# Thirteen dual products and four plain gate blocks in a gated convolution block: the lead computes products 1 and 2 of two duals

## The chip, the cores and the metric

The kernel runs on one core of a Trainium2 chip (trn2). The metric is the device time of one execution in microseconds (us); the time of a kernel is the median of several runs. Beside the runs stands one profiled execution, with a record of every instruction: TensorE (PE) does the matrix products and has its weight loads shown apart (PEld), VectorE (DVE), ScalarE (ACT) and GpSimd (POOL) work on elements, and the sync engine (SP) issues most transfers.

## The reference, cut to what matters

```python
h = rms_norm(x, norm_mix_g) * (1.0 + sc1) + sh1
proj = einsum('bsd,de->bse', h, w_in)            # 1024 x 1024 by 1024 x 7168
b_s, c_s, v_s, v_c, gl_c, gate_br = split(proj)  # 56 blocks of 128 columns
y_a = b_s * causal_dwconv(c_s * v_s, conv_short_w)          # width 3
u = v_c * sigmoid(gl_c)
u = causal_dwconv(u, conv_conf_w) + conv_conf_b             # width 31
g_a, g_b = split(sigmoid(gate_br))
...
```

After it come two projections, the gated merge, an output projection, a SwiGLU layer and a last norm. None of these is touched by the change. The stage in question is the input projection `proj`: 1024 tokens (two halves of 512), 1024 input channels (8 chunks of 128, `KC`), and 56 blocks of 128 output channels: 8 each of `bs`, `cc`, `vs`, `vc`, `gl`, and the gates `ga` and `gb`.

## The kernel before

All data stand channel-major: a tile has 128 channels on the partitions and 512 tokens. A float32 product is made of three matmuls of a rounded format: each operand is split into a rounded part and a rest (`wh`, `wl` of a weight; names ending in `h`, `l` of an operand), and `mm3` issues `wh` by `xh`, `wh` by `xl`, `wl` by `xh`. One such triple multiplies a 128 by 128 weight with 512 tokens. The rounded part is made on ScalarE (L226 for weights, L420, L470 for operands), the rest on VectorE or GpSimd (L227, L421, L471).

**The lead.** The first blocks of the projection run while the inputs are still being normalised. `row_blocks` keeps seven output banks open (`LEAD` = 7: three pairs `gl`, `vc` and the gate `gb` 0) and loops over the chunks k of the input. For each k, `act_x` loads two modulation rows (`modulation`, a VectorE reduction L361), scales x (`modulate`: VectorE L462, ScalarE L470 makes `hk0h`, VectorE L471 `hk0l`), and seven outputs get their products with that chunk. In the first half of the tokens (h = 0) chunks 0 to 2 are whole float32 products (`WHOLE` = 3, L376), and chunks 3 to 7 are triples, 21 matmuls a chunk. After chunk 6's second output the sum of squares of the second half, `ss`, is made on TensorE (`SUM_AT`, L540) from `squares_x` (ScalarE L525, VectorE L529); its reciprocal root scales the second half. The second half of the lead (h = 1) takes the chunks in the order 5, 6, 7, 0, 1, 2, 3, 4, with 7 x 3 matmuls a chunk. At the end of a half `glu` and `gate` empty the banks.

**One plain block** (`gb` 1, 48 matmuls) follows, by `col_block`.

**The duals.** The remaining 48 blocks are done in pairs, two pairs a dual (`PAIRS`), by a 2 by 2 scheme of Winograd's kind: seven products (`PRODUCTS` = "1265734", in this order) in place of eight. Products 1 and 2 use the plain operands (`th["1"]`, `th["2"]` are chunks 0 to 3 and 4 to 7 of the first half), the others sums and differences of operands (`t2`, `t`: VectorE L425, L712, L718, split by `t_split`) and of weights. One product is 2 output blocks x 4 chunks x 3 = 24 matmuls. The weights of a dual come from `dual_units`: all seven are split on GpSimd (wl, L227), and the four sums of weights are GpSimd's too. `win_evac` empties the banks; with it, eight 31-tap convolutions (`conv`, L915) run on VectorE, spread over `CONV_DUALS` duals.

What decides the order: the kernel is traced in program order, and a list scheduler with modelled times gives each engine one queue; `issue_after` adds edges to it. On the chip each queue is taken in its order, and an instruction waits for semaphores of others. `keep_clock` puts fillers on TensorE during the start (`CLOCK`). `raws` are five buffers for weight loads, in turn.

Of the kernel before, what the change touches and what calls it, by code (L numbers as in the profile page):

```python
# [40 lines left out]
P = 128  # L41
# [23 lines left out]

LEAD = 7
WHOLE = 3

CLOCK = (10, 3, (5,), 9, 5)

# [20 lines left out]
PAIRS = [  # L94
# [4 lines left out]
]  # L99


CONV_DUALS = 11

# [24 lines left out]
def block_kernel(ctx: ExitStack, tc: tile.TileContext, x0, xT, c, vecs, ada, w_first, w_plain, w_duals,  # L128
# [81 lines left out]
    def load(src, n=1024):  # L210
        raw = raw_tile(n)
        load.ins = nc.sync.dma_start(raw, src).ins
        return raw

    pool_los = []
# [81 lines left out]

    def apart_units(mats, eng):


        a = {}

        def add(out, x, y):
            eng.tensor_tensor(out, x, y, ALU.add)
            return out

        def get(b):
            return load(mats[("11", "12", "21", "22").index(b)])

        def unit(m):  # L310
            if m in "12":
                raw = get("1" + m)
            elif m == "6":
                for b in ("21", "22", "11"):
                    a[b] = get(b)
                a["s1"] = add(a["22"], a["21"], a["22"])
                raw = a["s2"] = add(raw_tile(), a["11"], a["s1"])
            elif m == "7":
                raw = add(a["21"], a["21"], a["11"])
# [5 lines left out]
            return split_w(raw, 1024, (), eng)  # L325
# [46 lines left out]
    def mm3(outs, wsl, w, xs, first, last, again=False):  # L372

        if w[1] is None:
            for ps, x in zip(outs, xs):
                mm3.ins = nc.tensor.matmul(ps, w[0][:, wsl], x, start=first, stop=last).ins  # L376
            return
        wh, wl = w[0][:, wsl], w[1][:, wsl]
        for ps, (xh, xl) in zip(outs, xs):
            nc.tensor.matmul(ps, wh, xh, start=first, stop=False, skip_group_check=again)  # L380
            nc.tensor.matmul(ps, wh, xl, start=False, stop=False, skip_group_check=again)  # L381
        for ps, (xh, _) in zip(outs, xs):
            mm3.ins = nc.tensor.matmul(ps, wl, xh, start=False, stop=last, skip_group_check=again).ins  # L383
# [113 lines left out]

    def row_blocks(act, n, name, ops, unit, joined=2):

# [3 lines left out]
        for k in range(KC):  # L503
# [51 lines left out]
    def glu(j, h, gl, vc):  # L555
        if h == 0:
            u.append(u_tile(j))
        sig = g_tile("sig")
        nc.scalar.activation(sig, gl, AF.Sigmoid)
        nc.vector.tensor_tensor(u[j][:, CK - 1 + h * H : CK - 1 + (h + 1) * H], vc, sig, ALU.mult)  # L560

# [84 lines left out]
    def act_x(k, h=0):  # L646
        nonlocal rx_0, rx_1
        if h == 0:
            with ExitStack() as after:
                after.enter_context(tc.issue_after(squares_x.ins[1] if k in (0, X1_AT + 2) else modulate.ins[0]))  # L650
                for i in range(2 * k, 2 * k + 2):
# [6 lines left out]
        hT[k][h] = modulate(x[k, h], rx_1 if h else rx_0, naff1[:, k : k + 1], modc(k),  # L658
                            None if whole else f"h{k}{h}", None if h else xin[k])
        if h == 0:  # L660
            if k == X1_AT:
                for i in range(KC):
                    x[i, 1] = s_tile(f"x{i}1")
                    nc.sync.dma_start(x[i, 1], xT[i, :, halves[1]])
            elif k == X1_AT + 1:
# [5 lines left out]
            if whole:  # L671
                return x[k, 0]
        elif k < WHOLE:
            hT[k][0] = split(x[k, 0], hl_tile, f"h{k}0")
        return hT[k][h]

    def sum_x1():
# [15 lines left out]
    rx_1 = None  # L693
    plan[:KC] = [lambda k=k: weights(w_first[k], LEAD * P, [modulate.ins[0]]) for k in SECOND[KEPT:]]
    ops = ()
    for h in range(2):
        lead = row_blocks(act_x if h == 0 else lambda i: act_x(SECOND[i], 1), LEAD, "lead", ops,
                          again_w if h else lead_w, 1 + h)
        if h == 0:
            ops = [(again_w(i), xs) for i, xs in ((i, act_x(SECOND[i], 1)) for i in range(2))]  # L700
        for j in range(LEAD // 2):
            glu(j, h, lead[2 * j], lead[2 * j + 1])
        gate("b", 0, h, lead[-1])


    KH = KC // 2
    th = {m: [None] * KH for m in PRODUCTS}
    t2 = []
    for k in range(KH):
        (b11, b12), (b21, b22) = ((x[i, 0], x[i, 1]) for i in (k, k + KH))  # L710
        th["1"][k], th["2"][k], th["3"][k] = hT[k][0], hT[k + KH][0], hT[k + KH][1]
        nc.vector.tensor_tensor(b11, b11, b12, ALU.subtract)  # L712
        t2 = hl_tile("t2", dt=F32)
        minus(t2, b11, b22)
        th["6"][k] = t_pair("t2")
        t_split(t2, *th["6"][k])
        minus(b21, t2, b21)
        nc.vector.tensor_tensor(b12, b22, b12, ALU.subtract)  # L718
    for h, ps in enumerate(col_block(next_w(), hT, (0, 1), "gb")):
        gate("b", 1, h, ps)  # L720
    for m, i, h in (("5", 0, 0), ("7", 0, 1), ("4", KH, 0)):
        for k in range(KH):
            th[m][k] = t_pair("t")
            t_split(x[k + i, h], *th[m][k])


# [19 lines left out]

    reads = [(0.0, t_split.ins)]

# [18 lines left out]
    def win_evac(d, pairs, banks):  # L767
# [23 lines left out]
        def read(i, m, ps):  # L791
            kind, j, *rest = pairs[i]
            e = st[i]
            if m in "165":
                if m == "5":
                    e["z"] = e["c"][1] if kind == "g" else g_tile("z")
                copy = nc.scalar.copy({"1": banks["y", i], "6": e.get("b", [0, 0])[1], "5": e.get("z")}[m], ps)
                if i:
# [42 lines left out]
        return evac  # L841


# [50 lines left out]
    TAPS = CK // 2 * 3 + 2  # L894

    def read_at(t):

        return max((r for r in reads if r[0] <= t), key=lambda r: r[0])[1]

    def conv(j):  # L900
# [3 lines left out]
        d, e = diff[:, :NE], diff[:, NE : 2 * NE - 1]  # L904
        with tc.issue_after(read_at(j * CONV_DUALS / KC)):
            nc.vector.tensor_tensor(d, ev, od, ALU.subtract)
# [4 lines left out]
        def tap(out, src, s, wt, acc):  # L911
            nonlocal n
            n += 1
            with tc.issue_after(read_at((j * TAPS + n) * CONV_DUALS / (KC * TAPS))):
# [4 lines left out]
        with tc.issue_after(read_at(j * CONV_DUALS / KC)):  # L919
            nc.vector.tensor_scalar(a0, od[:, :H], wsum[:, j : j + 1], col(V_CB, j), ALU.mult, ALU.add)  # L920
# [8 lines left out]
    def add_conv(j):  # L929

        hi, lo = pool_los[min(int((j + 1) * CONV_DUALS * 7 / KC) + 5, 7 * n_duals - 1)]
        with tc.issue_after(hi):
# [40 lines left out]

    n_duals = len(PAIRS) // 2
    ring = [[ps_tile("bank") for _ in range(2)] for _ in "xyz"]
    for d in range(n_duals):
        banks = {(b, p): ring[(d + i) % 3][p] for i, b in enumerate("xyz") for p in range(2)}
        evac = win_evac(d, PAIRS[2 * d : 2 * d + 2], banks)
        if d == n_duals - 1:
            q_steps.pop(0)()  # L980
        for i, m in enumerate(PRODUCTS):
            product(banks, m, th[m], evac, onto="2")
            if d == n_duals - 1:
                q_steps.pop(0)()
    while late:
# [564 lines left out]
```

## Time and profile before

| | |
|---|---|
| median of 3 runs | 1472.15 us (1470.73 to 1473.96) |
| the profiled execution | 1470.4 us, its span 1468.6 us |
| matmuls, VectorE, ScalarE, GpSimd instructions | 6443, 1627, 895, 464 |
| weights of the duals (`in_w_duals`) | 48 loads of 512 KB, 3.5 us each to landing |

The span is the time from the first to the last recorded instruction. The stretches are: start until 16 us, whole products of the lead to 34 us, the first half of the lead to 59 us, the second half to 97 us, the plain block to 108 us, and then the duals until about 565 us. In the rows of the timeline, columns are the start in us, the duration in us, engine, line, operation, output<-inputs, shapes and count; in square brackets stands the idle time of the engine before it and what ended it. A row with a count above 1 covers several instructions, and its duration reaches from the first one's start to the last one's end. "Windows" rows give the busy time of each engine with the number of instructions in a stretch, then the granted TensorE clock and the transfers.

### The profile page before, as it was taken

The page shows a single profiled execution, that of the slowest core. Times are in us where ns is not written, and L with a number is a line of the kernel's source. Part 1 is how long each engine was busy: PE and PEld are TensorE (multiplying, and loading weights), DVE is VectorE, ACT ScalarE, POOL GpSimd, SP SyncE. Part 2 cuts the span into 40 slices and gives each one's busy share as a digit, 9 for nine tenths or more (in the row PEclk, how much of TensorE's full clock was granted, in tenths as well). Part 3 has the DMA queues.
Part 4 walks back from the last instruction along what each step waited for, and adds up shares of the span by engine and source line. Part 5 has one row for each costly group of instructions (what it writes and reads, how often), then busy time and mean ns, then how long its engine had stood idle before and what let it go on. Part 6 is the DMA issues. An engine that isn't in the chain of part 4 may idle for free.

```text
span 1468.6 us, 17760 instructions
## 1 busy us (share of the span) xinstructions
PE 1457.7 (99%) x6443; PEld 1197.3 (82%) x6443; DVE 1179.1 (80%) x1627; ACT 615.4 (42%) x895; POOL 515.8 (35%) x464
## 2 busy tenths in 40 slices
PE   9999999999999999999999999999999999999997
PEld 5888888888888888888888888888888888888887
DVE  8999898887998969999688799776777665676755
ACT  4753333333433346455235475343444443222325
POOL 0046677767777771111022002110111015435005
PEclk9999999999999999999999999999999999999999
DMA  9412313222322258375586337655554449988403
GB/s 369 177 52 72 101 60 127 72 86 101 101 70 76 95 205 300 115 251 206 195 313 219 105 109 236 227 172 166 178 170 170 149 155 373 345 285 275 144 15 115
DMA packets 83913, 247.97 MB, mean 169 GB/s; under 512 B 9665, under 2 KB 11713, under 8 KB 83826
## 3 DMA queue, kind: packets, MB, share of 16 engines
q1 hardware_dynamic: 43072, 138.63, 27.5%
q0 software_dynamic: 37008, 95.63, 19.6%
q10 hardware_dynamic: 3746, 12.59, 2.3%
q8 instruction: 50, 0.82, 0.2%
q14 instruction: 37, 0.30, 0.1%
HBM read 184.41 MB, written 62.39 MB: 168 GB/s over the span
## 4 chain that ended last, share of the span: by engine, by line
PE 97%; DVE 1%; POOL 0%; issue 0%; ACT 0%; POOLq 0%; DVEq 0%
PE bank L380 12%; PE bank L383 12%; PE bank L381 12%; PE x L381 8%; PE x L383 8%; PE x L380 8%; PE z L381 4%; PE z L380 4%; PE z L383 4%; PE y L380 3%; PE y L381 3%; PE y L383 3%; PE mix L383 2%; PE yb L383 2%; PE yb L380 2%; PE mix L381 2%
## 5 line engine op out<-in xcount | busy, mean ns | idle before, releaser
L226 ACT CAST wh<-raw 128x1024 fp32r<-128x1024 f32 (+2 forms) x253 | 255.6, 1011 | 467.6 <-PE bank L381 126.8
L227 POOL TENSOR_TENSOR wl<-raw,wh 128x1024 fp32r<-128x1024 f32 x84 | 204.8, 2446 | 82.1 <-ACT wh L226 82.1
L227 DVE TENSOR_TENSOR wl<-raw,wh 128x1024 fp32r<-128x1024 f32 (+2 forms) x169 | 193.7, 1146 | 37.9 <-ACT wh L226 36.7
L915 DVE SCALAR_TENSOR_TENSOR c<-diff,vec,c 128x512 f32<-128x512 f32 x232 | 171.0, 753 | 4.4
L1263 POOL DMA_DIRECT2D hid<-stage x71 | 37.9, 534 | 346.0 <-DVE stage L421 341.5
L380 PE MATMUL bank<-th,wh 128*128 128x512 f32 x288 | 112.0, 389 | 0.0
L381 PE MATMUL bank<-tl,wh 128*128 128x512 f32 x288 | 112.0, 389 | 0.0
L383 PE MATMUL bank<-th,wl 128*128 128x512 f32 x288 | 112.0, 389 | 0.0
L915 DVE SCALAR_TENSOR_TENSOR c<-u,wsum,c 128x512 f32<-128x512 f32 x112 | 84.3, 753 | 2.6
L246 POOL TENSOR_TENSOR raw<-raw 128x1024 f32<-128x1024 f32 x12 | 29.2, 2431 | 124.1 <-DVE wl L227 86.9
L420 ACT CAST stage<-g 128x512 fp32r<-128x512 f32 x62 | 38.4, 622 | 72.8 <-DMA hid<-stage 39.6
L421 DVE TENSOR_TENSOR stage<-g,stage 128x512 fp32r<-128x512 f32 x62 | 42.5, 689 | 27.5 <-ACT stage L420 27.4
L383 PEld LDWEIGHTS bank<-th,wl 128*128 128x128 f32 x288 | 54.1, 188 | 11.3
L381 PEld LDWEIGHTS bank<-tl,wh 128*128 128x128 f32 x288 | 54.1, 188 | 11.2
L380 PEld LDWEIGHTS bank<-th,wh 128*128 128x128 f32 x288 | 54.1, 188 | 11.2
L1289 POOL DMA_DIRECT2D th<-hid x71 | 38.1, 537 | 53.6 <-PE x L383 32.7
L380 PE MATMUL x<-th,wh 128*128 128x512 f32 x144 | 56.1, 390 | 0.1
L383 PE MATMUL x<-th,wl 128*128 128x512 f32 x144 | 56.0, 389 | 0.0
L381 PE MATMUL x<-tl,wh 128*128 128x512 f32 x144 | 56.0, 389 | 0.0
L246 DVE TENSOR_TENSOR raw<-raw 128x1024 f32<-128x1024 f32 (+1 forms) x17 | 19.2, 1130 | 40.1 <-DMA raw<-in_w_fi 29.0
L380 PE MATMUL yb<-zsh,wh 128*128 128x512 f32 x128 | 49.8, 389 | 0.0
L381 PE MATMUL yb<-zsl,wh 128*128 128x512 f32 x128 | 49.8, 389 | 0.0
(812 smaller groups left out, 4243.2 us busy)
## 6 DMA issues: line engine op xcount, KB each, us to landing
hid<-stage POOLq DMA_DIRECT2D x71, 512.0 KB, 4.6
raw<-in_w_fi SPq DMA_DIRECT2D x54, 512.0 KB, 4.5
raw<-in_w_duals SPq DMA_DIRECT2D x48, 512.0 KB, 3.5
th<-hid POOLq DMA_DIRECT2D x71, 256.0 KB, 5.6
tl<-hid POOLq DMA_DIRECT2D x71, 256.0 KB, 5.6
ada<-in_ada SPq DMA_DIRECT2D x24, 512.0 KB, 5.9
raw<-in_ada SPq DMA_DIRECT2D x24, 512.0 KB, 4.8
raw<-in_w_fo SPq DMA_DIRECT2D x24, 384.0 KB, 5.8
```

The costliest lines, as they stand in the source:

```text
L226: hi = nc.scalar.copy(wh, raw)
L227: lo = lo_engine.tensor_tensor(wl, raw, f32(wh), ALU.subtract)
L246: eng.tensor_tensor(a["s1"], a["21"], a["22"], ALU.add)
L380: nc.tensor.matmul(ps, wh, xh, start=first, stop=False, skip_group_check=again)
L381: nc.tensor.matmul(ps, wh, xl, start=False, stop=False, skip_group_check=again)
L383: mm3.ins = nc.tensor.matmul(ps, wl, xh, start=False, stop=last, skip_group_check=again).ins
L420: t_split.act = nc.scalar.copy(hi, src).ins
L421: t_split.ins = nc.vector.tensor_tensor(lo, src, f32(hi), ALU.subtract).ins
L915: tap.ins = nc.vector.scalar_tensor_tensor(out=out, in0=src[:, s : s + H], scalar=wt, in1=acc, op0=ALU.mult, op1=ALU.add).ins
L1263: nc.gpsimd.dma_start(hid_dram[key], s)
L1289: nc.gpsimd.dma_start(t, hid_dram[key][:, s])
```

## The change

The lead has three gates (`gb` 0 to 2, `GATES` = 3) and, in the four further rows, the first two duals' output blocks of the first half: chunks 0 to 3 of such a row are product 1 of that dual, and all eight chunks products 1 and 2 together (`BEGUN` = 2). So with chunk 3 each of these four banks is stopped and copied by ScalarE into a tile `m1` (`half_way`, L835 of the changed kernel), and chunks 4 to 7 are added onto the bank. The second half of the lead has the three gate rows alone, 9 matmuls a chunk, and its weight loads are cut to 384 columns. `gb` 3 is the one plain block. There are 13 duals; duals 0 and 1 have only products 6, 5, 7, 3, 4 left, and their product 1 is copied from `m1` into the bank. The order of products is: 1 and 2 of dual 2, then 6, 5, 7, 3, 4 of duals 0, 1 and 2, then all seven of each further dual.

Weights of duals 0 to 2 come from `apart_units`: all of dual 0, and products 1 and 2 of dual 2, are on VectorE; the others on GpSimd, with the four sums in place in the loaded tiles. The differences of the second token half among the operands (L718 before) are made later, between the splits. The whole chunks' `h00`, `h10`, `h20` are split after the second half's chunks. `CLOCK`'s last filler count goes from 5 to 4. The convolutions are spread from dual 1.0 over 11.2 duals.

```diff
+GATES = 3
+BEGUN = 2
-CLOCK = (10, 3, (5,), 9, 5)
+CLOCK = (10, 3, (5,), 9, 4)
 PAIRS = [
-    ("p", 0), ("g", ("b", 2), ("b", 3)), ("p", 1), ("u", 3), ("q", 0), ("g", ("b", 4), ("b", 5)), ("p", 2), ("u", 4),
...
+    ("u", 0), ("u", 1), ("p", 0), ("p", 1), ("u", 2), ("p", 2), ("q", 0), ("u", 3), ("p", 3), ("g", ("b", 4), ("b", 5)),
...
-CONV_DUALS = 11
+CONV_FROM, CONV_DUALS = 1.0, 11.2
...
-    def apart_units(mats, eng):
+    def apart_units(mats, eng, on_eng=PRODUCTS, after=None):
...
+            unit.eng = eng if m in on_eng else nc.gpsimd
...
+                with tc.issue_after(after()) if after else ExitStack():
+                    a["s1"] = add(a["22"], a["21"], a["22"])
+                    if "6" in on_eng:
+                        raw = a["s2"] = add(raw_tile(), a["11"], a["s1"])
+                    else:
+                        a["s3"] = add(a["21"], a["21"], a["11"])
+                        raw = a["s2"] = add(a["11"], a["11"], a["s1"])
...
-    for d in range(len(PAIRS) // 2):
-        units = dual_units([w_duals[d, m] for m in range(4)], 1024, eng=nc.gpsimd)
-        plan += [units[m] for m in PRODUCTS]
+    win_units = [apart_units([w_duals[d, m] for m in range(4)], nc.vector, "12" if d else PRODUCTS,
+                             (lambda: t_split.ins) if d == 1 else None) for d in range(BEGUN + 1)]
+    win_units += [dual_units([w_duals[d, m] for m in range(4)], 1024, eng=nc.gpsimd) for d in range(BEGUN + 1, n_duals)]
+    win_order = [(BEGUN, m) for m in "12"] + [(d, m) for d in range(BEGUN + 1) for m in PRODUCTS[2:]]
+    win_order += [(d, m) for d in range(BEGUN + 1, n_duals) for m in PRODUCTS]
...
+                    half = half_way is not None and o >= whole
...
-                        mm3([outs[o]], slice(o * P, o * P + P), w, [xs], kk == 0, kk == KC - 1)
+                        mm3([outs[o]], slice(o * P, o * P + P), w, [xs], kk == 0, kk == KC - 1 or half and kk == KH - 1, half and kk >= KH)
+                    if half and kk == KH - 1:
+                        half_way(o - whole, outs[o])
...
+    def half_way(i, ps):
+        nc.scalar.copy(m1[i], ps)
...
-    ops = ()
-    for h in range(2):
-        lead = row_blocks(act_x if h == 0 else lambda i: act_x(SECOND[i], 1), LEAD, "lead", ops,
-                          again_w if h else lead_w, 1 + h)
...
+        lead = row_blocks(act_x if h == 0 else lambda i: act_x(SECOND[i], 1), GATES if h else LEAD, "lead", ops,
+                          again_w if h else lead_w, 1 + h, None if h else half_way, GATES)
...
+        for j, ps in enumerate(lead):
+            if j < GATES:
+                gate("b", j, h, ps)
+            else:
+                begun[(j - GATES) // 2]((j - GATES) % 2, "2", ps)
...
+    for p in range(2):
+        nc.scalar.copy(win_banks[0]["x", p], m1[p])
...
+            if m == "7" and k:
+                nc.vector.tensor_tensor(x[k, 1], x[k + KH, 1], x[k, 1], ALU.subtract)
...
+    for d, m in win_order:
...
+        product(win_banks[d], m, th[m], win_evacs[d], onto="2")
```

More of the change, by code (lines that the diff above doesn't have):

```diff
@@ L211, in load @@
         raw = raw_tile(n)
-        load.ins = nc.sync.dma_start(raw, src).ins
+        with tc.issue_after(x1_load[0]) if x1_load else ExitStack():
+            load.ins = nc.sync.dma_start(raw, src).ins
         return raw
+    x1_load = []
     pool_los = []
@@ L375, in mm3 @@
             for ps, x in zip(outs, xs):
-                mm3.ins = nc.tensor.matmul(ps, w[0][:, wsl], x, start=first, stop=last).ins
+                mm3.ins = nc.tensor.matmul(ps, w[0][:, wsl], x, start=first, stop=last, skip_group_check=again).ins
             return
@@ L650, in act_x @@
                 after.enter_context(tc.issue_after(squares_x.ins[1] if k in (0, X1_AT + 2) else modulate.ins[0]))
+                if k == X1_AT + 2:
+                    x1_load.append(act_x.last)
+                    after.enter_context(tc.issue_after(x1_load[0]))
                 for i in range(2 * k, 2 * k + 2):
@@ L657, in act_x @@
         whole = h == 0 and k < WHOLE
-        hT[k][h] = modulate(x[k, h], rx_1 if h else rx_0, naff1[:, k : k + 1], modc(k),
-                            None if whole else f"h{k}{h}", None if h else xin[k])
+        with tc.issue_after(los[-2]) if len(los) > 1 else ExitStack():
+            hT[k][h] = modulate(x[k, h], rx_1 if h else rx_0, naff1[:, k : k + 1], modc(k),
+                                None if whole else f"h{k}{h}", None if h else xin[k])
+        if h:
+            los.append(modulate.ins[2])
         if h == 0:
@@ L672, in act_x @@
                 return x[k, 0]
-        elif k < WHOLE:
-            hT[k][0] = split(x[k, 0], hl_tile, f"h{k}0")
         return hT[k][h]
+    los = []
     def sum_x1():
@@ L744, in short_conv @@
                 )
-    reads = [(0.0, t_split.ins)]
+    reads = []
     def plus(out, ps, b):
@@ L841, in win_evac @@
         return evac
+    plan[:KC] = [lambda k=k: weights(w_first[k][:, : GATES * P], GATES * P, [modulate.ins[0]]) for k in SECOND[KEPT:]]
+    win_banks = [{} for _ in range(BEGUN)]
+    begun = [win_evac(d, PAIRS[2 * d : 2 * d + 2], win_banks[d]) for d in range(BEGUN)]
+    m1 = diffp.tile([P, T + CK - 1], F32, tag="diff", name="m1")
+    m1 = [m1[:, s] for s in halves] + [s_tile("m1") for _ in range(2)]
+    def half_way(i, ps):
+        nc.scalar.copy(m1[i], ps)
+    ops = ()
+    for h in range(2):
+        lead = row_blocks(act_x if h == 0 else lambda i: act_x(SECOND[i], 1), GATES if h else LEAD, "lead", ops,
+                          again_w if h else lead_w, 1 + h, None if h else half_way, GATES)
+        if h == 0:
+            ops = [(again_w(i), xs) for i, xs in ((i, act_x(SECOND[i], 1)) for i in range(2))]
+        if h:
+            for k in range(WHOLE):
+                with tc.issue_after(modulate.ins[2]):
+                    hT[k][0] = split(x[k, 0], hl_tile, f"h{k}0")
+        for j, ps in enumerate(lead):
[3 more added lines that the diff above has]
+                begun[(j - GATES) // 2]((j - GATES) % 2, "2", ps)
@@ new lines, in block_kernel @@
+    th = {m: [None] * KH for m in PRODUCTS}
+    for k in range(KH):
+        (b11, b12), (b21, b22) = ((x[i, 0], x[i, 1]) for i in (k, k + KH))
+        th["1"][k], th["2"][k], th["3"][k] = hT[k][0], hT[k + KH][0], hT[k + KH][1]
+        nc.vector.tensor_tensor(b11, b11, b12, ALU.subtract)
+        t2 = hl_tile("t2", dt=F32)
+        minus(t2, b11, b22)
+        minus(b21, t2, b21)
+        if k == 0:
+            nc.vector.tensor_tensor(b12, b22, b12, ALU.subtract)
+        th["6"][k] = t_pair("t2")
+        t_split(t2, *th["6"][k])
@@ new lines, in block_kernel @@
+    x1_load.clear()
+    for h, ps in enumerate(col_block(next_w(), hT, (0, 1), "gb")):
+        gate("b", GATES, h, ps)
+    fetch(AHEAD + 1)
+    ring = [[ps_tile("bank") for _ in range(2)] for _ in "xyz"]
+    for n, banks in enumerate(win_banks):
+        banks.update({(b, p): ring[i][p] for b, i in (("x", n), ("z", 1 - n)) for p in range(2)})
+    for p in range(2):
+        nc.scalar.copy(win_banks[0]["x", p], m1[p])
+    for m, i, h in (("5", 0, 0), ("7", 0, 1), ("4", KH, 0)):
+        for k in range(KH):
+            if m == "7" and k:
+                nc.vector.tensor_tensor(x[k, 1], x[k + KH, 1], x[k, 1], ALU.subtract)
+            th[m][k] = t_pair("t")
+            t_split(x[k + i, h], *th[m][k])
@@ L844, in block_kernel @@
+    reads.append((0.0, t_split.ins))
     tq = {m: [None] * KH for m in PRODUCTS}
@@ L972, in ln_rstd @@
         return [rstd_end(*r) for r in rs]
[L974 to L978, printed above, removed]
+    win_banks.append({(b, p): ring[i][p] for b, i in (("x", 2), ("y", 1), ("z", 0)) for p in range(2)})
+    win_banks += [{(b, p): ring[(d + i) % 3][p] for i, b in enumerate("xyz") for p in range(2)}
+                  for d in range(BEGUN + 1, n_duals)]
+    win_evacs = begun + [win_evac(d, PAIRS[2 * d : 2 * d + 2], win_banks[d]) for d in range(BEGUN, n_duals)]
+    for d, m in win_order:
+        if d == n_duals - 1 and m == PRODUCTS[0]:
+            q_steps.pop(0)()
+        if d + 1 < BEGUN and m == PRODUCTS[-1]:
+            for p in range(2):
+                nc.scalar.copy(win_banks[d + 1]["x", p], m1[2 * (d + 1) + p])
+        product(win_banks[d], m, th[m], win_evacs[d], onto="2")
         if d == n_duals - 1:
             q_steps.pop(0)()
[L981 to L984, printed above, removed]
     while late:
@@ L1515 @@
     bs, cc, vs, vc, gl, ga, gb = ([8 * n + m for m in j] for n in range(7))
-    n = LEAD // 2
-    lead = [b for m in j[:n] for b in (gl[m], vc[m])] + gb[:1]
     at = {"u": lambda m: (vc[m], gl[m]), "p": lambda m: (cc[m], vs[m]), "q": lambda m: (bs[m], bs[m + 1]),
@@ L1520 @@
     pairs = [at[kind](*a) for kind, *a in PAIRS]
+    lead = gb[:GATES] + [row for row, _ in pairs[: 2 * BEGUN]]
     w_fi, w_fo = i["w_ffn_in"][0], i["w_ffn_out"][0]
```

61 lines of the change are left out of this document (18 added, 43 removed), and 4 rows, old and new, of the table PAIRS.

## The prediction

> **What bounds the kernel now.** I read the page first, then the busy time by stretches, then the timeline of each engine between 30 and 112 us, where the change works.
>
> ```profile
> span 1468.6 us, 17760 instructions
> PE 1457.7 (99%) x6443; PEld 1197.3 (82%) x6443; DVE 1179.1 (80%) x1627; ACT 615.4 (42%) x895; POOL 515.8 (35%) x464
> ...
> PE 97%; DVE 1%; POOL 0%; issue 0%; ACT 0%; POOLq 0%; DVEq 0%
> ```
>
> TensorE is busy for 99% of the span, and 97% of the chain of waits is its own. So a matmul less is worth its whole slot, and any wait of TensorE costs its whole length.
>
> ```profile
> 34.00:60.00 26.00, 26.00 (x113) 21.03 (x112) 24.81 (x44) 17.43 (x28) 0.00 (x0) 1.00 0.63 242
> 60.00:100.00 40.00, 40.00 (x178) 33.12 (x177) 38.01 (x52) 25.18 (x39) 6.59 (x3) 1.00 0.23 73
> 300.00:400.00 100.00, 100.00 (x442) 82.80 (x442) 84.22 (x122) 37.78 (x53) 73.83 (x33) 1.00 0.30 100
> ```
>
> The columns are the stretch, its length, and the busy time of PE, PEld, DVE, ACT and POOL. A matmul's slot is 100.00 / 442 = 0.226 us. Between 34 and 100 us VectorE is busy 62.8 of 66 us: TensorE is full, but VectorE is nearly full beside it, and it feeds TensorE.
>
> **Part 1, matmuls removed.** In units of 12 matmuls (one output block, four chunks, one token half), the lead's second half loses four of seven rows: 4 x 2 = 8 units. The duals' part was 12 x 14 units and is now 2 x 10 + 11 x 14 = 174, 6 more. The plain block stays. So 2 units, 24 matmuls: 24 x 0.226 = 5.4 us less. The filler less in `CLOCK` is one slot, and it stands just ahead of the first product, which waits for x as well: 0 to 0.2 us, I take 0.2.
>
> **Part 2, the copies into `m1`.** These are four ScalarE copies of 128x512 from a bank, each waiting for the twelfth matmul of its row, which is the last one of chunk 3. What matters is where they stand. In the built program of the changed kernel, ScalarE's queue reads:
>
> ```
> wh (chunk 5)
> m1 <- lead3
> m1 <- lead4
> m1 <- lead5
> m1 <- lead6
> h40h
> wh (chunk 6)
> ...
> ```
>
> Before, `h40h` stood behind `wh` of chunk 4. So now chunk 4's rounded operand is made only after the last row of chunk 3 has ended and been copied.
>
> ```profile
> 31.82 0.72 ACT L470 ACTIVATE h40h<-x,mod 128x512 fp32r<-128x512 f32 x1 [1.49 <-DVE x L462]
> ...
> 111.17 0.57 ACT L797 COPY bank<-bank 128x512 f32<-128x512 f32 x1 [0.40 <-ACT sig L564]
> ```
>
> ```profile
> 38.72 0.39 PE L383 MATMUL lead<-h30h,wl 128*128 128x512 f32 x1
> 38.95 0.39 PE L380 MATMUL lead<-h40h,wh 128*128 128x512 f32 x1
> ...
> 49.60 0.39 PE L383 MATMUL lead<-h60h,wl 128*128 128x512 f32 x1
> 49.83 0.59 PE L540 MATMUL ss<-sq,ones 128*128 128x512 f32 x1
> ...
> 54.13 0.84 PE L380 MATMUL lead<-h70h,wh 128*128 128x512 f32 x3
> ...
> 58.89 0.39 PE L380 MATMUL lead<-h51h,wh 128*128 128x512 f32 x1
> ```
>
> The last matmul of chunk 3 ends at 38.72 + 0.39 = 39.1; the copy takes 0.57 and `h40h` 0.72, so `h40h` is there at 40.4 and not at 32.5. TensorE wants it at 38.95: a wait of 1.5 us.
>
> That is the smaller half. Behind `h40h` waits `h40l` on VectorE, and behind that, in order, all that VectorE has to do for chunks 5, 6, 7 and the second token half.
>
> ```profile
> 31.03 0.75 DVE L462 SCALAR_TENSOR_TENSOR x<-x,naff,rx0r 128x512 f32<-128x512 f32 x1
> 32.70 0.74 DVE L471 SCALAR_TENSOR_TENSOR h40l<-x,mod,h40h 128x512 fp32r<-128x512 f32 x1
> 37.64 0.75 DVE L471 SCALAR_TENSOR_TENSOR h50l<-x,mod,h50h 128x512 fp32r<-128x512 f32 x1
> 42.57 0.74 DVE L471 SCALAR_TENSOR_TENSOR h60l<-x,mod,h60h 128x512 fp32r<-128x512 f32 x1
> 44.63 4.67 DVE L529 TENSOR_TENSOR sq<-sq 128x512 f32<-128x512 f32 x6 [0.40 <-ACT sq L525]
> 53.49 0.74 DVE L471 SCALAR_TENSOR_TENSOR h70l<-x,mod,h70h 128x512 fp32r<-128x512 f32 x1
> ```
>
> `h40l` starts at 40.45 in place of 32.70: VectorE's chain is 7.75 us late, and its steps are its own work (4.94 and 4.93 us from one `hl` to the next, 6.73 from `h60l` to the end of the sums at 49.30, 4.19 from there to `h70l`), so it stays late. Now TensorE against it, with 21 matmuls (4.76 us) a chunk:
> - chunk 4 runs from 40.5 to 45.2. `h50h` needs x of chunk 5, late by the same 7.75: a wait of about 0.1, then to 50.1.
> - `h60h` and `h60l` (50.3 + 0.74): waits of 0.2 and 0.45. Then six matmuls, until 52.2.
> - `ss` stands there in TensorE's queue, as before. Its sums end at 49.30 + 7.75 = 57.05. Before, TensorE came 0.5 us after them; now it waits 57.05 - 52.2 = 4.9 us.
> - `ss` and the rest of chunk 6 last until 61.4 (54.13 - 49.83 = 4.30 before), `h70l` ends at 53.49 + 7.75 + 0.74 = 62.0: 0.5.
>
> Sum for the first half: 1.5 + 0.1 + 0.65 + 4.9 + 0.5 = 7.7 us. If the copies held nothing up, it would be 0.
>
> **Part 3, the second half of the lead.** TensorE has 18 matmuls (4.1 us) on chunks 5 and 6, then 9 (2.0 us) a chunk, where it had 42 and 21. ScalarE has in its queue, between `h51h` and `h71h`, the table load, three sigmoids and four copies that empty the seven banks, `h61h` and two others of 128x512.
>
> ```profile
> 55.02 1.28 ACT L559 ACT_TABLE_LOAD   x1
> 56.31 0.60 ACT L559 ACTIVATE sig<-lead 128x512 f32<-128x512 f32 x1
> 56.81 0.71 ACT L470 ACTIVATE h51h<-x,mod 128x512 fp32r<-128x512 f32 x1
> ```
>
> A sigmoid takes 0.50 to the next start, an `h51h` 0.61: 1.28 + 7 x 0.50 + 3 x 0.61 = 6.6 us, about 7.8 with the small waits for VectorE, against 4.1. Waits between 0 (TensorE's lateness covers them) and 7.8 - 4.1 = 3.7; I count 0.2 for the bank, 0.6 and 0.6 for `h61h` and `h61l`, 0.9 for `h71h`: 2.3, nearest to what the queue holds. From then on VectorE needs about 1.8 us a chunk (x, `hl`, the cut weights) against TensorE's 2.0: no wait.
>
> **Part 4, dual 0's weights on VectorE and the operand differences.** Five splits and four sums of dual 0 and two splits of dual 2 move from GpSimd to VectorE.
>
> ```profile
> 85.11 0.69 DVE L425 SCALAR_TENSOR_TENSOR t<-x,x 128x512 f32<-128x512 f32 x1
> 88.50 1.22 DVE L227 TENSOR_TENSOR wl<-raw,wh 128x1024 fp32r<-128x1024 f32 x1
> ...
> 100.82 9.66 DVE L421 TENSOR_TENSOR tl<-x,th 128x512 fp32r<-128x512 f32 x4 [1.60 <-ACT th L420]
> ```
>
> ```profile
> 85.88 0.62 ACT L420 CAST t2h<-t 128x512 fp32r<-128x512 f32 x1 [2.27 <-DVE t L425]
> ...
> 87.42 1.05 ACT L226 CAST wh<-raw 128x1024 fp32r<-128x1024 f32 x1 [0.40 <-PE lead L381]
> ```
>
> A split is 1.2; a sum has the split's shape, and I take 1.1 for it: 7 x 1.2 + 4 x 1.1 = 12.8 us more on VectorE, in the stretch where it is at 95%, while TensorE's work ahead of product 6 shrinks from 264 matmuls (168 + 48 + 48) to 168. In the built queue two matmuls of product 6 stand even after the first 12 of dual 2's product 1. TensorE is there at 66.6 (58.9 + 7.7) + 2.3 + 132 x 0.226 = 98.7. What it needs, `wh` of product 6, stands on ScalarE behind the fourth `t2`. Before, `h70l` to the fourth `t2` took 85.11 - 53.49 = 31.6 us; now without three products of `glu` (1.8), three later differences (1.8) and half of five weight splits (2.7), with two sums, the plain block's split and two of dual 2 (2 x 1.1 + 3 x 1.2), and some 5.5 us of waiting for ScalarE in part 3: 36.6, from 61.2 to 97.8. `t2` 0.7, `t2h` 0.6, `wh` 1.05: 100.2 to 100.5. A wait between 0 and 3; I take 1.6. Later products have 5.4 us each against some 5 us of VectorE's splits: 0. The four `tl` of the last row took 2.4 us each where they met GpSimd's sums; with dual 0's sums gone from GpSimd they should take about 0.7, but TensorE was full there, so that gain is nothing but cover.
>
> **Part 5, all else.** GpSimd and VectorE keep some 26 and 16 us of every 100 free in the duals (row of 300 to 400): the shifted convolutions cost 0 there; without that cover each bank read late would hold a product.
>
> **The sum.** Profiled execution 1470.4 - 5.4 - 0.2 + 7.7 + 2.3 + 1.6 = 1476.4; the median shown stands 1.75 above that execution, so 1478.
>
> **The rivals.**
> 1. *The gain alone.* The copies don't hold `h40h`: TensorE stays full, 1472.15 - 5.6 = 1466.5. For it: TensorE never waits there before, with 6 us to spare on `h40h`. Against: that spare is VectorE's lead, and it is just what the queue's order gives away. It decides if `h40h` still runs before 38 us.
> 2. *Late, but only once.* The first half loses 7.7 us, and parts 3 and 4 are covered: 1472.15 - 5.6 + 7.7 = 1474.2.
> 3. *The clock falls in the wait.* When the last matmuls end, the granted clock goes down:
>
> ```profile
> 1462.00:1464.00 2.00, 0.00 (x0) 0.00 (x0) 1.56 (x5) 0.37 (x1) 1.26 (x2) 1.00 0.37 131
> 1464.00:1466.00 2.00, 0.00 (x0) 0.00 (x0) 0.75 (x2) 0.00 (x0) 0.84 (x2) 0.62 0.84 297
> ...
> 1458.48 1.89 PE L1450 MATMUL ss<-sq,ones 128*128 128x256 f32 x8
> ```
>
> 0.62 in a stretch that ends at 0.5 puts the step near 1464.5, 4.1 us after TensorE's end at 1460.4; a wait of 4.9 would reach it. The fillers at the start show the way back:
>
> ```profile
> 1.62 4.63 PE L573 MATMUL clock<-ones_r 128*128 128x512 f32 x10 [1.62 <-DVE ones_r L591]
> ...
> 11.67 2.64 PE L573 MATMUL clock<-ones_r 128*128 128x512 f32 x9
> ```
>
> (4.63 - 0.39) / 9 = 0.47 us a matmul there, 0.28 later. Some 5 us at half speed lose 2.5 us, of which parts 3 and 4 give back about 1: 1478 + 1.5 = 1479.5.
>
> The Trainium skill's page "TensorE: Matmul & The Clock Gate", section "Part 1: The HAM clock gate (the "warmup" mystery)", says that the gate goes to half rate after an idle window of about 3.4 us that runs free of the kernel. By it a wait of 4.9 us holds a whole window in (4.9 - 3.4) / 3.4, about 4 of 10 executions; the 4.1 us above agree.
>
> 4. *GpSimd comes early.* If its first sums for dual 1 start while VectorE still has some eight `tl` to make, each takes 2.4 in place of 0.7: 8 x 1.7 = 14 us, about 8 of it beyond the spare time of products 7, 3 and 4: 1486. Against: GpSimd's buffers are freed only by VectorE's splits of dual 0.
>
> **How the numbers follow.** Forecast 0.45, rival 1 0.11, rival 2 0.13, rival 3 0.23, rival 4 0.08. The predicted time is the forecast's, 1478, with its own range of 1475.5 to 1481. The range goes from 1471, which takes in rival 2 and leaves rival 1 out, to 1484, which takes in rival 3 and leaves rival 4 out. A change of 0.2%, 2.9 us, is about what can be told from none. Faster: rival 1, 0.11. Same: most of rival 2 and the low edge of the forecast, 0.12. Slower: 0.77.
>
> **What would show it.** In the profile after: `h40h` at about 39.7 behind four L835 copies; TensorE idle 1.5 us near 39 and 4 to 5 us ahead of `ss`, released by VectorE's `sq`; VectorE idle some 7.8 us ahead of `h40l`; small waits on `h61h` and `h71h`; one wait for `wh` near 100 us; 24 matmuls fewer in `proj`, at the same 0.226 us. The clock's digits near 57 us decide rival 3. I am wrong if TensorE shows no idle time between 38 and 60 us, or if stretches after 150 us differ.

## The result, and the profile after

| | before | after |
|---|---|---|
| median | 1471.44 us (4 runs, 1470.22 to 1473.96) | 1479.82 us (4 runs, 1479.28 to 1480.62) |
| profiled execution | 1470.4 us, span 1468.6 us | 1480.1 us, span 1478.3 us |

The changed kernel takes 1.0055 times as long, with a 95% interval of 1.0038 to 1.0073. It is slower by 8.4 us, although TensorE has less to do. The page of the changed kernel, its first lines:

```profile
span 1478.3 us, 17762 instructions
...
PE 1456.7 (99%) x6418; PEld 1192.3 (81%) x6418; DVE 1181.8 (80%) x1642; ACT 625.5 (42%) x911; POOL 506.6 (34%) x460
```

There are 25 matmul records fewer (6443 before): the 24 of the projection and one filler. The timeline of ScalarE and VectorE in the changed kernel shows the place that the prediction named:

```profile
38.11 2.62 ACT L835 COPY m<-lead 128x512 f32<-128x512 f32 x4 [3.53 <-PE lead L397]
40.63 0.72 ACT L484 ACTIVATE h40h<-x,mod 128x512 fp32r<-128x512 f32 x1
...
41.39 0.75 DVE L485 SCALAR_TENSOR_TENSOR h40l<-x,mod,h40h 128x512 fp32r<-128x512 f32 x1 [7.93 <-ACT h40h L484]
...
53.32 4.67 DVE L546 TENSOR_TENSOR sq<-sq 128x512 f32<-128x512 f32 x6 [0.39 <-ACT sq L542]
```

ScalarE stood idle for 3.53 us with the copies at its head, and all of them were done before `h40h` could start. VectorE stood idle for 7.93 us ahead of `h40l`; nothing behind it in the queue ran before it. The sums of squares end at 57.99 in place of 49.30. TensorE's timeline of the changed kernel, its waits and the first matmul of each stretch:

```profile
17.11 1.48 PE L390 MATMUL lead<-x,raw 128*128 128x512 f32 x3
34.77 0.79 PE L394 MATMUL lead<-h30h,wh 128*128 128x512 f32 x1
41.41 0.50 PE L394 MATMUL lead<-h40h,wh 128*128 128x512 f32 x1 [1.30 <-ACT h40h L484]
52.06 0.50 PE L395 MATMUL lead<-h60l,wh 128*128 128x512 f32 x1 [0.17 <-DVE h60l L485]
58.14 1.19 PE L557 MATMUL ss<-sq,ones 128*128 128x512 f32 x1 [4.86 <-DVE sq L546]
64.09 0.39 PE L394 MATMUL lead<-h70h,wh 128*128 128x512 f32 x1
68.85 0.39 PE L394 MATMUL lead<-h51h,wh 128*128 128x512 f32 x1
73.60 0.50 PE L394 MATMUL lead<-h71h,wh 128*128 128x512 f32 x1 [0.35 <-ACT h71h L484]
86.12 0.39 PE L394 MATMUL gb<-h00h,wh 128*128 128x512 f32 x1
97.83 0.39 PE L394 MATMUL bank<-h00h,wh 128*128 128x512 f32 x1
102.04 0.50 PE L394 MATMUL bank<-t2h,wh 128*128 128x512 f32 x1 [1.33 <-ACT wh L231]
160.53 0.50 PE L397 MATMUL bank<-th,wl 128*128 128x512 f32 x1 [0.61 <-POOL wl L232]
573.65 0.39 PE L394 MATMUL bank<-q1h,wh 128*128 128x512 f32 x1
625.65 0.50 PE L397 MATMUL bank<-q6h,wl 128*128 128x512 f32 x1 [0.52 <-DVE wl L232]
```

The same points of the kernel before, to measure against (`q1h` is the first product after the input projection):

```profile
16.15 18.18 PE L376 MATMUL lead<-x,raw 128*128 128x512 f32 x42
33.77 0.79 PE L380 MATMUL lead<-h30h,wh 128*128 128x512 f32 x1
...
564.81 0.39 PE L380 MATMUL bank<-q1h,wh 128*128 128x512 f32 x1
```

A bracket shows a single wait; the length of a stretch, from one first matmul to the next, shows all of them. The first half from `h30h` to `h51h` takes 34.08 us in place of 25.12, 8.96 more. The waits in it are 1.30, 0.17 and 4.86. From `ss` to `h70h` there is no wait, and yet that piece takes 5.95 us where it took 4.30. The windows of the changed kernel say why (columns as in the prediction; the granted clock is the third number from the end):

```profile
57.50:58.00 0.50, 0.00 (x0) 0.00 (x0) 0.50 (x2) 0.00 (x0) 0.00 (x0) 1.00 0.00 0
58.00:58.50 0.50, 0.36 (x1) 0.39 (x2) 0.50 (x1) 0.00 (x0) 0.00 (x0) 0.51 0.00 0
58.50:61.00 2.50, 2.50 (x5) 1.27 (x5) 2.47 (x7) 0.69 (x1) 0.00 (x0) 0.50 0.00 0
61.00:61.50 0.50, 0.50 (x3) 0.40 (x2) 0.50 (x2) 0.20 (x1) 0.00 (x0) 0.58 0.00 0
```

The clock fell to half at 58.0, just as TensorE came back to work, and stayed there for 3.4 us. The third rival's event happened.

### The profile page after: what moved, and what is told of

The parts are those of the page before. It is cut to its first block, busy times and chain, and to the rows that moved or that the text cites. A ratio compares the mean times of both kernels' runs of the same rounds, so it can differ in the third digit from the quotient of the medians.

```text
span 1478.3 us, 17762 instructions
## 1 busy us (share of the span) xinstructions
PE 1456.7 (99%) x6418; PEld 1192.3 (81%) x6418; DVE 1181.8 (80%) x1642; ACT 625.5 (42%) x911; POOL 506.6 (34%) x460
## 4 chain that ended last, share of the span: by engine, by line
PE 81%; issue 4%; DVE 2%; POOL 2%; DMA 1%; ACT 0%; POOLq 0%; DVEq 0%
PE bank L397 9%; PE bank L395 9%; PE bank L394 9%; PE x L395 7%; PE x L397 7%; PE x L394 7%; PE z L394 4%; PE z L395 4%; PE z L397 4%; PE y L394 3%; PE y L397 3%; PE y L395 3%; PE mix L397 2%; PE mix L394 2%; PE yb L394 2%
## 5 line engine op out<-in xcount | busy, mean ns | idle before, releaser
L231 ACT CAST wh<-raw 128x1024 fp32r<-128x1024 f32 (+3 forms) x256 | 256.9, 1005 | 461.5 <-PE bank L395 143.9
L232 DVE TENSOR_TENSOR wl<-raw,wh 128x1024 fp32r<-128x1024 f32 (+3 forms) x176 | 200.6, 1140 | 47.6 <-ACT wh L231 46.5
L232 POOL TENSOR_TENSOR wl<-raw,wh 128x1024 fp32r<-128x1024 f32 x80 | 194.4, 2432 | 104.0 <-ACT wh L231 103.8
L397 PE MATMUL bank<-th,wl 128*128 128x512 f32 x312 | 121.5, 389 | 0.6 <-POOL wl L232 0.6
L394 PE MATMUL bank<-th,wh 128*128 128x512 f32 x312 | 121.4, 389 | 0.0
L395 PE MATMUL bank<-tl,wh 128*128 128x512 f32 x312 | 121.4, 389 | 0.0
L397 PEld LDWEIGHTS bank<-th,wl 128*128 128x128 f32 x312 | 58.6, 188 | 13.1 <-POOL wl L232 1.0
L394 PEld LDWEIGHTS bank<-th,wh 128*128 128x128 f32 x312 | 58.6, 188 | 12.2
L309 POOL TENSOR_TENSOR raw<-raw 128x1024 f32<-128x1024 f32 x8 | 20.1, 2509 | 121.0 <-DMA raw<-in_w_duals 117.1
L397 PE MATMUL yb<-zsh,wl 128*128 128x512 f32 x128 | 49.8, 389 | 0.0
```

The lines of the kernel that those rows point to most:

```text
L231: hi = nc.scalar.copy(wh, raw)
L232: lo = lo_engine.tensor_tensor(wl, raw, f32(wh), ALU.subtract)
L309: unit.eng.tensor_tensor(out, x, y, ALU.add)
```

## The experiments

Times of experiments stand beside runs of the kernel before on the same chip: 1471.54 us (21 runs) for the first four, 1470.93 us (17 runs) for the others.

**1. The copies behind `h40h`.** Same copies, traced after chunk 4's operand and ahead of the matmuls that add onto the bank:

```diff
                     half = half_way is not None and o >= whole
+                    if half and kk == KH:
+                        half_way(o - whole, outs[o])
                     ...
-                    if half and kk == KH - 1:
-                        half_way(o - whole, outs[o])
```

> The changed kernel, with the four copies into m1 traced one step later, so that they stand behind h40h in ScalarE's queue, though still ahead of h50h. Theory (the queue position of the copies makes VectorE's chain 8 us late, and the rest follows): h40l is no longer late, h50h waits for the last copy instead, VectorE's chain is about 2.8 us late at h50l; TensorE waits about 2.3 us ahead of ss and 0.6 ahead of h70l, the clock does not fall, product 6 starts about 5 us earlier: about 1474.5 us against the changed kernel's 1479.8. Rival A (the chain of the second half and of the t2 operands sets the time, not the copies): within 1 us of 1479.8. Rival B (the copies were all that was wrong): the 5.4 us of matmuls show, about 1467.

Measured: 1474.60 us (ratio 1.0019, 1.0010 to 1.0027); the theory had 1474.5. In this kernel's timeline of TensorE one wait is left in the first half:

```profile
52.16 0.83 PE L557 MATMUL ss<-sq,ones 128*128 128x512 f32 x1 [2.22 <-DVE sq L546]
```

The 2.3 us foreseen there came as 2.22, and product 6 starts at 95.86, 62.1 us after `h30h` in place of 67.3. The expectation erred in two points: the clock fell here too (see the last section), and the 0.6 us ahead of `h70l` did not show. So the total was met with two errors in it.

**2. The copies behind `h50h` as well.** Chunk 5's operand is traced one chunk earlier:

```diff
-            if k == len(ops):
-                xs = act(k)
-                ops.append((unit(k), xs))
+            while len(ops) <= k + (half_way is not None and k == KH):
+                xs = act(len(ops))
+                ops.append((unit(len(ops)), xs))
```

> The changed kernel, with chunk 5's operand traced ahead of the copies too, so that all four copies stand behind h50h. Theory: no wait of TensorE between 34 and 60 us, no wait ahead of ss; VectorE's chain as before the change, some 8 us earlier than in the changed kernel; behind it the chain of the second half and of t2 stays as it is and bounds product 6, which starts near 94 us (102.0 in the changed kernel): about 1472 us, level with the kernel before. Rival A (copies do not matter): 1479.8. Rival B (TensorE stays full to the end of the projection): 1466.5.

Measured: 1469.81 us (ratio 0.9989, 0.9980 to 0.9998): faster than the kernel before by 1.7 us. Its windows and its one wait at product 6:

```profile
34.00:60.00 26.00, 25.87 (x110) 20.23 (x109) 24.29 (x45) 18.38 (x30) 0.00 (x0) 1.00 0.62 229
```

```profile
93.89 0.50 PE L394 MATMUL bank<-t2h,wh 128*128 128x512 f32 x1 [1.31 <-ACT wh L231]
```

TensorE is busy for 25.87 of 26 us (19.67 in the changed kernel), the clock stays at 1.00, and product 6 starts at 93.89, where 94 was expected. The 10.0 us between this and the changed kernel are the price of the order: the same instructions, with `h40h` and `h50h` ahead of the copies. In the profiles, 8.2 us of it are there by product 6 (93.89 against 102.04). The theory's total of 1472 was 2 us too high.

**3. The copies alone, in the kernel before.** Four copies into an unused tile after chunk 3 are added, and the four rows end their sum there so that they can be copied. The scheduler moved one modulation reduction ahead of `h40l` with it (33.13 us in VectorE's timeline), not the two that the expectation counts:

```diff
+    def half_way(i, ps):
+        nc.scalar.copy(m1[i], ps)
 ...
+                    if half and kk == KH - 1:
+                        half_way(o - whole, outs[o])
```

> The kernel before, with nothing but the four ScalarE copies of rows 3 to 6 after chunk 3 (their target is not used). They stand ahead of wh of chunk 6 and h40h in ScalarE's queue; two of the modulation reductions move ahead of h40l on VectorE, which takes 2.5 us off the lateness. Theory: h40h at about 41, TensorE waits about 2 us there, 3 us ahead of ss, 1 us for h60 and h70, no fall of the clock or a short one; nothing is given back, since the second half has 21 matmuls a chunk: about 1471.4 + 6 = 1477.5 us (1475 to 1480). Rival (four copies cost at most their own 2.3 us of ScalarE, which is idle there): 1471 to 1472.

Measured: 1480.43 us (ratio 1.0057, 1.0043 to 1.0071), 8.9 us slower for 2.3 us of copies on an engine that is busy 42% of the time. TensorE in this kernel:

```profile
41.89 0.50 PE L380 MATMUL lead<-h40h,wh 128*128 128x512 f32 x1 [2.13 <-ACT h40h L470]
...
57.60 0.67 PE L543 MATMUL ss<-sq,ones 128*128 128x512 f32 x1 [2.90 <-DVE sq L532]
```

Both waits are as expected (2 and 3 us); the 1 us for `h60` and `h70` did not show as waits. The time went over the top of the range by 0.4, and the clock fell after the first wait, which the expectation had left open:

```profile
42.50:43.00 0.50, 0.50 (x4) 0.41 (x3) 0.50 (x2) 0.34 (x1) 0.00 (x0) 0.97 1.08 415
43.00:46.00 3.00, 3.00 (x9) 2.32 (x8) 3.00 (x8) 1.10 (x2) 0.00 (x0) 0.50 1.05 405
46.00:46.50 0.50, 0.50 (x3) 0.40 (x2) 0.50 (x2) 0.00 (x0) 0.00 (x0) 0.62 0.95 365
```

**4. Fillers in the wait.** The changed kernel, with 14 matmuls of a constant ahead of `ss`:

```diff
+    def warm_tile(name):
+        t = ps2_tile(name)
+        for _ in range(14):
+            nc.tensor.matmul(t, ones_r[:, :P], ones_r, start=True, stop=True)
+        return t
...
-            rx_1 = rstd_square(norm_start(rx_1, "rx1", ss_tile=ps2_tile))
+            rx_1 = rstd_square(norm_start(rx_1, "rx1", ss_tile=warm_tile))
...
```

One edge more holds the gates' sigmoids behind `h51h`. In the profiles of this kernel and of the changed one, ScalarE's order from `h51h` on is the same.

> The changed kernel, with 14 filler matmuls of a constant ahead of ss, in the wait of 4.9 us (14 x 0.227 = 3.2 us); their result is overwritten. Theory (the clock fell in the wait and cost 1.65 us between ss and h70h, but the later chain of ScalarE and VectorE gives most of it back): the granted clock stays at 1.0 from 58 to 62 us, ss to h70h takes 4.3 us in place of 5.95, the waits of the second half grow by about 1.3, and product 6 starts at most 0.5 us earlier: 1479.3 to 1479.8 us. Rival (the clock's cost is on the path in full): 1478.1 us. Rival (fillers delay ss): 1480 to 1482.

Measured: 1479.57 us (ratio 1.0051, 1.0038 to 1.0064), against 1.0055 for the changed kernel: no difference that these runs can tell. TensorE's timeline of this kernel:

```profile
57.44 1.12 PE L557 MATMUL ss<-sq,ones 128*128 128x512 f32 x2 [1.61 <-DVE sq L546]
61.84 0.84 PE L394 MATMUL lead<-h70h,wh 128*128 128x512 f32 x3
...
67.15 0.50 PE L394 MATMUL lead<-h51h,wh 128*128 128x512 f32 x1 [0.38 <-ACT sig L574]
68.37 0.49 PE L394 MATMUL lead<-h61h,wh 128*128 128x512 f32 x1 [0.26 <-ACT h61h L484]
69.15 0.50 PE L395 MATMUL lead<-h61l,wh 128*128 128x512 f32 x1 [0.29 <-DVE h61l L485]
...
101.26 0.50 PE L394 MATMUL bank<-t2h,wh 128*128 128x512 f32 x1 [1.31 <-ACT wh L231]
```

The clock stays up: `ss` to `h70h` takes 4.40 us in place of 5.95. Three waits that are not marked in the changed kernel's profile appear behind it, ahead of `h51h`, `h61h` and `h61l`. This execution began 0.64 us earlier than that of the changed kernel (its `h30h` is at 34.13), and product 6 starts 0.78 us earlier, so 0.14 us of 1.55 were kept. In these profiles the fall of the clock cost almost nothing by product 6, since ScalarE and VectorE set the time behind it. The medians, 0.25 us apart, cannot tell so small a cost from none.

**5. Product 6 behind all of products 1 and 2.** Experiment 2's kernel with one edge more:

```diff
-        product(win_banks[d], m, th[m], win_evacs[d], onto="2")
+        with tc.issue_after(mm3.ins) if (d, m) == (0, "6") else ExitStack():
+            product(win_banks[d], m, th[m], win_evacs[d], onto="2")
```

> The version with the copies behind h50h (1469.8 us), with one edge more: the first two matmuls of product 6 of dual 0, which stood behind 12 matmuls of dual 2's product 1, now stand behind all 48 of its products 1 and 2. Theory (TensorE waits 1.3 us there only because those two matmuls stand early; what they need is there long before the 36 others are done): no wait for t2 near 94 us, nothing lost later: 1469.8 - 1.3 = 1468.5 us. Rival A (VectorE's chain sets the time behind it: the wait comes back ahead of product 5 or 7): 1469.8. Rival B (the other banks aren't free at once): 1469 to 1470.

Measured: 1469.40 us (ratio 0.9985, 0.9976 to 0.9994). The wait is gone from the profile (the next one of TensorE is 0.43 us at 148), and in this execution, whose `h30h` stands at 33.65, product 6 follows without a gap. The medians moved by less than the 1.3 us expected, and the intervals overlap, so the size of this gain is not shown.

**6. The second half repaired too.** On top of that, the table load moves behind the first reciprocal root, the four evacuation copies stand behind `h71h`, and the plain block takes the late-split chunks last:

```diff
+        with tc.issue_after(rstd_square.ins):
+            nc.scalar.activation(cp.tile([P, 1], F32, name="sg"), ones[:, :1], AF.Sigmoid)
...
+    def act_2(i):
+        xs = act_x(SECOND[i], 1)
+        if i == KEPT - 1:
+            with tc.issue_after(modulate.ins[1]):
+                empty(half_0)
+        return xs
...
-        for k in range(KC):
-            mm3(outs, slice(k * P, k * P + P), w, [act[k][h] for h in hs], k == 0, k == KC - 1)
+        for i, k in enumerate([*range(WHOLE, KC), *range(WHOLE)]):
+            mm3(outs, slice(k * P, k * P + P), w, [act[k][h] for h in hs], i == 0, i == KC - 1)
```

> On top of the last one, three repairs of the second half: the table load for the sigmoid stands where ScalarE is idle (a sigmoid of one column behind the first reciprocal root), the four evacuation copies of the lead stand behind h71h, and the plain block takes the chunks 3 to 7 first and the late-split 0 to 2 last. Theory: the waits for h71h and its neighbours (0.9 us from h51h to the plain block) and for h10l, h20l (0.8 us) go, 1.7 us in all: 1468.5 - 1.7 = 1466.8 us, which is the kernel before less its 24 matmuls. Rival A (VectorE is full from 74 to 102 us; TensorE arriving earlier waits for t2 or a weight there): 1468.5. Rival B (banks freed later hold the plain block): 1469 to 1471.

Measured: 1467.75 us (ratio 0.9981, 0.9970 to 0.9992), the fastest of all, 3.2 us ahead of the kernel before. Its windows:

```profile
34.00:60.00 26.00, 25.86 (x112) 20.66 (x111) 23.46 (x45) 19.03 (x31) 0.00 (x0) 1.00 0.57 208
60.00:100.00 40.00, 40.00 (x177) 32.75 (x176) 37.52 (x56) 31.40 (x52) 0.00 (x0) 1.00 0.46 149
```

TensorE is full from 60 to 100 us. The step from the last kernel, 1.65 us between medians, lies inside the intervals; that this kernel beats the one before does not. The profiles show less of a step: `q1h` stands at 560.89 here and at 561.13 in experiment 5, with `h30h` at 33.65 in both. The moved table load (1.28 us, at 52.13) is not in an idle place: it stands ahead of `h70h`, which starts at 53.53 in place of 52.14, and the first half takes 25.58 us in place of 25.13.

**7. Dual 0's weights back on GpSimd.** The changed kernel, with VectorE left only products 1 and 2 of dual 2:

```diff
-    win_units = [apart_units([w_duals[d, m] for m in range(4)], nc.vector, "12" if d else PRODUCTS,
+    win_units = [apart_units([w_duals[d, m] for m in range(4)], nc.vector, "12",
...
```

An index (`lo_at`) that places transfers of the convolutions by GpSimd's splits is moved to fit the five splits more.

> The changed kernel, with products 6, 5, 7, 3, 4 of dual 0 back on GpSimd: four sums and five splits of 128x1024, VectorE keeps products 1 and 2 of dual 2. Theory (GpSimd takes 2.45 us a sum or split, so product 6 needs 9.8 us from its loads, and VectorE's tl that meet them take 2.4 us in place of 0.7; here there are twelve tl and TensorE has no work in store): slower than the changed kernel, by 3 to 7 us: 1483 to 1487. Rival (VectorE is the bound from 84 to 102 us, and 3.6 us of work taken off it brings product 6 forward): 1476 to 1478.

Measured: 1491.46 us (ratio 1.0131, 1.0115 to 1.0147), 11.6 us above the changed kernel. It is slower, as expected, and 4.5 us over the top of the range. The profiled execution is the slowest of the four (1495.75 us). VectorE and GpSimd in this kernel, then TensorE:

```profile
86.27 2.88 DVE L427 TENSOR_TENSOR h10l<-x,h10h 128x512 fp32r<-128x512 f32 x1
89.68 3.38 DVE L232 TENSOR_TENSOR wl<-raw,wh 128x1024 fp32r<-128x1024 f32 x1
92.99 2.82 DVE L427 TENSOR_TENSOR h20l<-x,h20h 128x512 fp32r<-128x512 f32 x1
...
86.19 2.41 POOL L309 TENSOR_TENSOR raw<-raw 128x1024 f32<-128x1024 f32 x1 [83.28 <-DMA raw<-in_w_duals]
106.44 8.75 POOL L232 TENSOR_TENSOR wl<-raw,wh 128x1024 fp32r<-128x1024 f32 x1 [7.18 <-ACT wh L231]
```

```profile
95.86 0.76 PE L395 MATMUL gb<-h20l,wh 128*128 128x512 f32 x1 [5.00 <-DVE h20l L427]
115.24 0.79 PE L397 MATMUL bank<-t2h,wl 128*128 128x512 f32 x1 [6.40 <-POOL wl L232]
```

What was missed: the sums meet not the `tl` but, as soon as their loads land at 86, the late splits `h10l` and `h20l`, which TensorE waits for at once. The steps that take 0.7 or 1.2 us alone take 2.8 to 3.4 beside a sum, and one GpSimd split shows 8.75 us beside VectorE's steps from 106 to 113 us (spans on GpSimd are rough). The Trainium skill's page "SBUF — State Buffer", section "SBUF: two separate sides", states that VectorE and GpSimd share one pair of ports as an exclusive lock, held for a whole instruction; these rows agree with it. The edit also makes product 6 wait for GpSimd's own split (6.40), and the clock falls after the long waits; the shares of the 11.6 us are not separated.

## Why the prediction was right, point by point

The profiled span grew by 9.7 us; 6.0 were forecast. The steps, measured from first matmul to first matmul:

| step of the prediction | forecast | measured |
|---|---|---|
| 24 matmuls less | -5.4 | -5.4 (the slot is the same, experiment 6 keeps most of it) |
| start, with the filler | -0.2 | +1.0 (first product at 17.11, before at 16.15) |
| first half: `h40h` | 1.5 | 1.30 |
| `h60h`, `h60l` and the like | 0.75 | 0.17, and some 1.0 in small pieces |
| `ss` | 4.9 | 4.86 |
| `h70l` | 0.5 | 0 |
| the clock | 0 (rival 3: 2.5) | 1.65 |
| second half | 2.3 | 0.9 (68.85 to 86.12, less 72 x 0.227) |
| plain block | 0 | 0.8 (86.12 to 97.83, less 48 x 0.227) |
| product 6 | 1.6 | 1.5 (97.83 to 102.04, less 12 x 0.227) |
| later waits | 0 | 0.6 at 160, 0.5 at 626 |

The first half lost 8.96 us, and its named rows make 7.98; the other 1.0 are the small pieces. With them the measured column adds up to 8.9, and some 0.8 us of the 9.7 were not traced.

*The matmuls.* Right. Experiment 6, with nearly all waits gone, is 3.2 us ahead in the median and 4.0 in the profiled span (1464.6), of 5.6 foreseen without any wait; its wait of 0.55 us for GpSimd near 148 us and the longer first half are part of the rest.

*The copies' place.* Right in mechanism and in size. The queue was read from the built program, and lateness was carried from `h40l` to the end of the sums by VectorE's own work: 8.69 us late at the end of the sums (57.99 against 49.30), of which 0.96 is the later start of the whole kernel: 7.73, and 7.75 were foreseen. Experiments 1 and 2 move the copies behind one and two operand casts and take back 5.2 and 10.0 us. Experiment 3 adds the copies to the kernel before and loses 8.9.

*The clock.* The forecast left it up and gave the fall to rival 3. The fall came, after less of a wait than the 4.1 us that rival 3 read, and for 3.4 us where it took some 5: 1.65 us in place of 2.5. Rival 3 let later parts give back about 1 of its 2.5 us; here nearly all came back: experiment 4 keeps the clock up and shows no gain. It also explains the second half. Between `h51h` and the plain block the fillers' kernel loses 2.56 us (66.60, where TensorE was ready, to 85.49, less 16.33), close to the 2.3 of part 3, where the changed kernel loses 0.9: the same waits, hidden behind a later TensorE. So in the profiles the fall adds 0.14 us by product 6. The 1479.5 that rival 3 named stands close to the measured 1479.82 by luck: the rest came from the terms below.

*The terms that were wrong.* The start: a load of x came in later in this execution, and ScalarE's squares waited for it:

```profile
8.58 2.40 ACT L542 ACTIVATE sq<-x 128x512 f32<-128x512 f32 x4 [0.51 <-DMA x<-in_x]
```

The change doesn't touch that load, and the start differs between the profiles of the experiments, which share its code (`h30h` at 33.65 to 34.95). The filler was costed at a gain of 0.2, and no such gain shows. The plain block: part 4 costed the whole chunks' splits only as work on VectorE. They also have a due time, because the block takes chunks 0 to 2 first, and `h10l` and `h20l` came too late for it. The later waits had no term. Start, plain block and later waits (1.2, 0.8 and 1.1) come to 3.1 of the 3.7 us by which the profiled span was missed; the clock's 1.65 and small pieces came on top, and the second half, 1.4 too dear in the forecast, took some back. The median was missed by only 1.8, which is in part luck.

*The weights on VectorE.* Part 4 called the gain from GpSimd's absence "nothing but cover", since it looked at four `tl` for which TensorE did not wait. Experiment 7 shows the whole move to be worth 11.6 us: without dual 0 on VectorE, the change would have been far slower. That was not seen, though rival 4 had steps slowed beside GpSimd's sums.

## What to carry to other kernels

An instruction that waits for a late producer holds everything behind it in its engine's queue, and the loss is set by what stands behind it and not by its own length: 2.3 us of copies on an engine that was mostly idle cost 10 us, and all of it came back when the copies were put behind two operand casts. When work is added, look at what the built queue puts behind it, and follow that lateness through the other engines to the place where the busiest one meets it. A gain in TensorE's work only shows when the engines that feed it have spare time in that stretch, so the feeders' windows are to be read first.

## What was not expected of the hardware

The clock falls after waits much shorter than 4 us. In experiment 1 a wait of 2.22 us was enough, in experiment 3 one of 2.13, while one of 2.90 in the same execution was not. The windows of experiments 1 and 3, around the falls (at 52.5 and 43.0) and around the wait of 2.90:

```profile
49.10:52.50 3.40, 1.18 (x5) 0.67 (x4) 3.09 (x5) 1.65 (x3) 0.00 (x0) 1.00 0.00 0
55.50:56.00 0.50, 0.50 (x3) 0.41 (x2) 0.50 (x1) 0.50 (x2) 0.00 (x0) 0.54 0.00 0
```

```profile
39.57:42.97 3.40, 1.27 (x6) 0.90 (x6) 1.10 (x2) 2.49 (x5) 0.00 (x0) 1.00 1.03 410
...
53.20:56.60 3.40, 1.50 (x7) 0.92 (x5) 2.98 (x5) 2.15 (x5) 0.00 (x0) 1.00 0.02 6
56.60:60.00 3.40, 2.40 (x9) 1.71 (x10) 3.26 (x8) 0.69 (x1) 0.00 (x0) 1.00 0.00 0
```

Each of these spells at half speed lasts 3.4 us (52.5 to 56.0, 43.0 to 46.4, 58.0 to 61.4 in the changed kernel). If windows of 3.4 us are laid end to end from the fall of experiment 3, the wait of 2.90 is split over two of them, with TensorE busy for 1.50 and 2.40 us, and there is no fall. The windows that end at a fall have it busy for 1.18 and 1.27 us, and for none in the changed kernel. So a window need not be empty. Experiment 7 shows that the busy time alone doesn't draw the limit. Its windows, laid in the same way:

```profile
51.56:54.97 3.41, 1.71 (x6) 0.75 (x5) 2.82 (x9) 3.41 (x8) 0.00 (x0) 1.00 0.19 58
55.00:58.40 3.40, 0.07 (x1) 0.10 (x1) 2.99 (x5) 1.90 (x4) 0.00 (x0) 0.50 0.00 0
...
89.10:92.52 3.42, 1.65 (x6) 1.05 (x6) 3.42 (x3) 0.00 (x0) 3.28 (x2) 1.00 0.34 131
92.52:95.92 3.40, 0.06 (x1) 0.06 (x1) 3.40 (x3) 0.00 (x0) 2.74 (x1) 1.00 0.48 143
```

After a window with 1.71 us of work the clock is down, and after one with 1.65 it is not, nor after the one with 1.50 in experiment 3. The ends of matmuls are modelled in the records, and the limit was not tested by itself: it stays open.

The Trainium skill's page "TensorE: Matmul & The Clock Gate", section "Part 1: The HAM clock gate (the "warmup" mystery)", gives windows of about 3.4 us that run free of the kernel. The length of the spells agrees, and its "idle window" turns out here to be one with up to 1.71 us of work.
